# Last recurrent head: projection steps ahead of the masked copies, a later transposition of values, and a slab for the second half of the keys

## The chip, the cores and the metric

The kernel runs on one core of one Trainium2 chip. The metric is the device time of one execution in microseconds. Three runs of the kernel before took 1207.51, 1208.60 and 1209.41 us; the median is 1208.6 us. The profile is of one further execution.

## The reference, cut to what matters

One decoder layer over 1024 tokens and 1024 channels, in float32. The normed input goes through one projection `w_in`. Half of its output feeds a dilated attention of 8 heads of 64 channels, the other half a gated recurrence of 4 heads of 128 channels. Both are concatenated, go through `w_out`, and a two-layer MLP follows.

```python
proj = h @ w_in[layer]
q_a, k_a, v_a, q_h, f_h, i_h, g_h = jnp.split(proj, splits, axis=-1)
attn = dilated_mixture_attention(q_a..., k_a..., v_a..., slopes)
rec = hgrn2_recurrence(q_h, f_h, i_h, g_h, lower_bounds[layer], hgrn_out_norm[layer])
mixed = jnp.concatenate([attn, rec], axis=-1) @ w_out[layer]
```

The recurrence is, per head, `S_t = diag(f_t) S_{t-1} + (1-f_t) i_t^T` and `o_t = S_t^T q_t`, computed in chunks.

## The kernel before, in words

Every float32 matrix product is made in three passes: each operand is split into a high part (a rounding copy on ACT, `L86`) and a low part (a subtraction on DVE, `L87`), and `three_pass` issues high x low, high x high and low x high (`L90` to `L92`). So one contraction step of 128 is three matmuls of 512 columns. Below, one such step with its three matmuls is called a unit. The code counts it as 650.

The core works through the recurrent heads 0 to 3 (`hgrn_core`), then through the 64 steps of the attention's 8 heads, then through `w_out` and the MLP. All instructions stand in the order in which the code is written; each engine takes its own in that order, and a semaphore holds an instruction until what it needs is there. To keep PE busy in the recurrent heads, projections that later work needs are put between the pieces of a head. They are Python generators in `queue`; `fill(ns)` draws units from them until their costs reach `ns` (a debt is carried on), so the number in `fill` sets how many units are written at that place. In the last head (`h == 3`) the queue holds `attn_proj(0)` and `attn_proj(1)`, the projections of the first two pairs of attention heads: queries in two halves (`pm_aq`), the first half of the values (`pm_av`), both halves of the keys (`pm_ak`), the second half of the values. What a unit draws with it also goes to the other engines: at a half's end DVE reads the sum out of PSUM (`qf` at `L786`, `vf` at `L803`, `kf` at `L720`), ACT and POOL make its high and low part (`both_parts`: `hiq` or `hik`, then the subtraction in place), and SP's queue sends them on. At the fifth unit of a half of the queries, or of the values, the next weights are split, `wh` on ACT and `wl` on DVE.

`hgrn_core` itself: a prologue fills, makes sums `pd` on PE and their diagonal blocks in `at` on DVE. Then come three steps. Each step has 32 short matmuls into two banks `pl` (`L535`), a chain of updates on DVE (`qt` at `L548` and `L551`, totals at `L555` to `L557`, the next step's `qs` at `L490` and `L492`, `kt` at `L560` to `L562`), six masked copies of `pl` into `at` on DVE (`L567`), a fill of 3500 and another of 3500. The next step's `pl` needs the chain's `qs` and `kt`, not the copies; `at` is first needed after the third step. After that come `pl` 6 (`L578`), the turning of `kt` (`pk`), the states (`pu`) and the output (`po`).

`values_turn` transposes a half of the values on PE (`pvt`, `L753`), ACT and DVE copy the result into `v`, and SP stores it. For the first half of a pair's values it is drawn with the fourth unit of the first half of the keys (`n == 3` in `attn_proj`).

Buffers: PSUM has two banks per tag, and a projection's sum and `pvt` share tag `mm`. `half` is a slab of 512 columns with two buffers, for `qf`, `hiq`, `vf`, `kf` and `hik` alike. `kf` and `hik` of the first pair are free again only when the DMAs that read them have landed. Tag `P` has three buffers of 1024 columns.

After the recurrent heads the attention's 64 steps draw units by a table (`UNITS`), and at step 47 what is left of the queue is drained.

Of the kernel before, what the change touches and what calls it, by code (L numbers as in the profile page):

```python
# [9 lines left out]
F32R = mybir.dt.float32r  # L10
# [7 lines left out]
P = 128  # L18
# [8 lines left out]
HH = 4  # L27
# [10 lines left out]
def hymba_layer(ctx, tc, x, w_in, w_out, w_ff1, w_ff2, g_pre, lb_logits, g_mix, g_post,  # L38
# [464 lines left out]
    def hgrn_core(h, scale, after=None):  # L503
        hd = heads[h]
        inat, gate, prod, qt, kt, tot = (hd[n] for n in ("inat", "gate", "prod", "qt", "kt", "tot"))
        ready = quarter_sets(hd, h, 0, tot)
        fill((5900 if 0 < h < HH - 1 else 5200) * scale)
        at = slab("S", f"at{h}", F32, (P, NT, P))
        for hf in range(2):
            pd = bank("pv", f"pd{h}_{hf}")  # L510
# [14 lines left out]
        for step in range(3):  # L525
            c = 4 ** step
            nb = 32 // c
            sets, cv = ready
            got = []
            for u in range(2):  # L530
                pl = bank(("s", "t", "pv")[step], f"pl{h}_{step}{u}").rearrange("p (n q) -> p n q", n=4)
                for n in range(4):
                    qs = sets[u][:, n].rearrange("p (s w) -> p s w", s=3)
                    for g, (a, b) in enumerate(halves):
                        TE.matmul(pl[a:b, n, :96], kt[:, (4 * u + n) * P + a:(4 * u + n) * P + b],  # L535
                                  qs[:, :, 32 * g:32 * g + 32], start=True, stop=True, skip_group_check=True)
                got.append(pl)
            w = T // (4 * c)
            at_ = (0, 768, 960)[step]
            tots = totals[:, at_:at_ + 3 * w].rearrange("p (i w) -> p i w", i=3)  # L540
            u23, u123, nx = (tots[:, i] for i in range(3))
            cw = cv.rearrange("p n b f -> p (n b) f")
            q4 = qt.rearrange("p (m f c) -> p m f c", f=4, c=c)
            k4 = kt.rearrange("p (m f c) -> p m f c", f=4, c=c)

            def spread(ap, k=c):
                return ap.unsqueeze(2).to_broadcast([P, w, k])
            V.tensor_tensor(out=q4[:, :, 1], in0=q4[:, :, 1], in1=spread(cw[:, :, 0]), op=ALU.mult)  # L548
            for hf in range(2):
                n4 = slice(hf * 4, hf * 4 + 4)  # L550
                V.tensor_tensor(out=qt[:, hf * 512:hf * 512 + 512].rearrange("p (n b f c) -> p n b (f c)", n=4, f=4, c=c)  # L551
                                [:, :, :, 2 * c:],
                                in0=sets[hf][:, :, 128:].rearrange("p n (b w) -> p n b w", b=nb),
                                in1=cv[:, n4, :, 0:1].to_broadcast([P, 4, nb, 2 * c]), op=ALU.mult)
            V.tensor_tensor(out=u23, in0=cw[:, :, 2], in1=cw[:, :, 3], op=ALU.mult)  # L555
            V.tensor_tensor(out=u123, in0=cw[:, :, 1], in1=u23, op=ALU.mult)
            V.tensor_tensor(out=nx, in0=cw[:, :, 0], in1=u123, op=ALU.mult)  # L557
            if step < 2:
                ready = quarter_sets(hd, h, step + 1, nx)
            V.tensor_tensor(out=k4[:, :, 2], in0=k4[:, :, 2], in1=spread(cw[:, :, 3]), op=ALU.mult)  # L560
            V.tensor_tensor(out=k4[:, :, 1], in0=k4[:, :, 1], in1=spread(u23), op=ALU.mult)
            V.tensor_tensor(out=k4[:, :, 0], in0=k4[:, :, 0], in1=spread(u123), op=ALU.mult)  # L562
            for u, pl in enumerate(got):
                for part_, mask, c2 in ((0, own[:, 2 * step], c), (2, own[:, 2 * step + 1], 2 * c),
                                        (1, near[:, step], 2 * c)):
                    av = at[:, 4 * u:4 * u + 4, :64].rearrange("p n (b two c) -> p n b two c", two=2, c=c2)
                    V.copy_predicated(  # L567
                        av[:, :, :, 1, :],
                        mask.rearrange("p (b c) -> p b c", c=c2).unsqueeze(1).to_broadcast([P, 4, 32 // c2, c2]),
                        pl[:, :, part_ * 32:part_ * 32 + 32].rearrange("p n (b c) -> p n b c", c=c2))  # L570
            cur = nx
            table_part()
            fill(3500 * scale)
            table_part()
            fill(3500 * scale)
        pl = bank("s", f"pl{h}_6")
# [131 lines left out]
    turn_later = []  # L708
    second_done = [False] * (AH // 2)

    def both_parts(full, name):
        hi = half(f"hi{name}", F32R)
        S.activation(hi, f32(full), AF.Copy)
        G.tensor_tensor(out=full, in0=f32(full), in1=f32(hi), op=ALU.subtract)
        return hi, full

    def keys_read(pr, pm, hf):
        sl = slice(hf * 512, hf * 512 + 512)
        full = half(f"kf{pr}{hf}", F32R)
        V.tensor_tensor(out=f32(full).rearrange("p (r m) -> p r m", r=DIL), in0=classes(pm),  # L720
                        in1=rrow[:, sl].rearrange("p (r m) -> p r m", r=DIL), op=ALU.mult)
        keys_done[pr] += 1
        if pr > 0:
            key_jobs.extend((pr, i, hf, full) for i in range(2))
            return
        for q, src in zip(("kh", "kl"), both_parts(full, f"k{pr}{hf}")):
            for i, (a, b) in enumerate(halves):
                dst = f32(pairs[pr][0][i][q]).rearrange("p (r m) -> p r m", r=DIL)[:, :, hf * P:(hf + 1) * P]
                for c, d in halves:
# [35 lines left out]
    def attn_proj(pr):  # L765
# [50 lines left out]
        pairs[pr] = (stacks, vs)  # L816
        for hf in range(2):
            for n, cost in enumerate(proj_t(wk, f"ak{pr}", hf, box)):
                if n == 3 and hf == 0:
                    values_turn()  # L820
                    cost += 450.0
                yield cost
# [1469 lines left out]
```

## Time and profile before

| | |
|---|---|
| median of 3 runs | 1208.6 us |
| profiled execution, its own time | 1209.69 us |
| span from first to last instruction | 1207.9 us |
| mean granted TensorE clock | 0.997 |
| PE / DVE / ACT / POOL busy | 98% / 69% / 45% / 25% of the span |
| recurrent head 3 from `pd` to its last fill | about 240 to 303 us |
| the attention's steps | from about 304 us |

The profile counts time from the first instruction. In the windows of the trace, "PE busy" is the time in which a matmul is in flight, "PEclk" the granted clock as a share of full speed. In the timeline a row is start, duration, engine, line, operation, output from inputs, shapes, count, and in brackets how long the engine had been idle just before and whose end it had waited for. A matmul of 512 columns lasts 0.39 us there but overlaps its neighbours, so the distance between starts is the cost.

### The profile page before, as it was taken

The page shows a single profiled execution, that of the slowest core. Times are in us where ns is not written, and L with a number is a line of the kernel's source. Part 1 is how long each engine was busy: PE and PEld are TensorE (multiplying, and loading weights), DVE is VectorE, ACT ScalarE, POOL GpSimd, SP SyncE. Part 2 cuts the span into 40 slices and gives each one's busy share as a digit, 9 for nine tenths or more (in the row PEclk, how much of TensorE's full clock was granted, in tenths as well). Part 3 has the DMA queues.
Part 4 walks back from the last instruction along what each step waited for, and adds up shares of the span by engine and source line. Part 5 has one row for each costly group of instructions (what it writes and reads, how often), then busy time and mean ns, then how long its engine had stood idle before and what let it go on. Part 6 is the DMA issues. An engine that isn't in the chain of part 4 may idle for free.

```text
span 1207.9 us, 17596 instructions
## 1 busy us (share of the span) xinstructions
PE 1186.9 (98%) x6486; PEld 1008.7 (84%) x6486; DVE 838.9 (69%) x1426; ACT 548.4 (45%) x1082; POOL 296.9 (25%) x284
## 2 busy tenths in 40 slices
PE   9999999979999999999999999999999999999997
PEld 8898989857888888888888888888888888888886
DVE  5686969574666767676689566766678553578796
ACT  7633433332565668755664222232234543434562
POOL 0121212001120110143320786575631000000022
PEclk9999999999999999999999999999999999999999
DMA  5222333125645455272514555553586534533337
GB/s 217 71 67 84 97 96 97 53 82 125 147 107 134 123 147 160 56 242 105 192 62 157 183 210 190 194 190 144 198 323 264 196 105 139 169 93 105 105 105 279
DMA packets 90549, 175.49 MB, mean 145 GB/s; under 512 B 14944, under 2 KB 42464, under 8 KB 90464
## 3 DMA queue, kind: packets, MB, share of 16 engines
q1 hardware_dynamic: 90320, 174.37, 44.9%
q8 instruction: 51, 0.84, 0.3%
q14 instruction: 34, 0.28, 0.1%
q10 hardware_dynamic: 144, 0.00, 0.0%
HBM read 116.91 MB, written 47.99 MB: 137 GB/s over the span
## 4 chain that ended last, share of the span: by engine, by line
PE 89%; DVE 5%; ACT 3%; issue 1%; DMA 1%; SPq 0%; POOL 0%; DVEq 0%; POOLq 0%; ACTq 0%
PE f L2032 18%; PE f2s L2032 7%; PE pig L90 2%; PE pig L92 2%; PE pig L91 2%; PE pwo L90 2%; PE pwo L92 2%; PE pwo L91 2%; PE pl L535 1%; PE pm_aq L92 1%; PE pm_ak L90 1%; PE pm_q L90 1%; PE pm_aq L90 1%; PE pm_ak L91 1%; PE pm_ak L92 1%
## 5 line engine op out<-in xcount | busy, mean ns | idle before, releaser
L87 DVE TENSOR_TENSOR al<-ar,ah 128x1024 fp32r<-128x1024 f32 x56 | 70.6, 1261 | 80.0 <-ACT ah L86 77.6
L2032 PE MATMUL f<-bh,ah 128*128 128x512 f32 x320 | 124.5, 389 | 0.0
L2032 PE MATMUL f<-bl,ah 128*128 128x512 f32 x320 | 124.5, 389 | 0.0
L2032 PE MATMUL f<-bh,al 128*128 128x512 f32 x320 | 124.5, 389 | 0.0
L86 ACT ACTIVATE ah<-ar 128x1024 fp32r<-128x1024 f32 x56 | 59.1, 1056 | 86.6 <-DMA ar<-actd 86.3
L2032 PEld LDWEIGHTS f<-bh,ah 128*128 128x128 f32 x320 | 60.1, 188 | 12.6
L2032 PEld LDWEIGHTS f<-bl,ah 128*128 128x128 f32 x320 | 60.1, 188 | 12.5
L2032 PEld LDWEIGHTS f<-bh,al 128*128 128x128 f32 x320 | 60.1, 188 | 12.3
L2106 POOL TENSOR_SCALAR lbl<-ssq 128x1 f32<-128x1 f32 x4 | 3.3, 821 | 245.0 <-ACT fd L2102 244.8
L1655 POOL TENSOR_TENSOR e<-x,e 128x512 f32<-128x512 f32 x14 | 21.6, 1541 | 131.8 <-DVE x L1606 131.8
L2032 PE MATMUL f2s<-bl,ah 128*128 128x512 f32 (+1 forms) x128 | 48.9, 382 | 0.0
L2032 PE MATMUL f2s<-bh,al 128*128 128x512 f32 (+1 forms) x128 | 48.9, 382 | 0.0
L2032 PE MATMUL f2s<-bh,ah 128*128 128x512 f32 (+1 forms) x128 | 48.9, 382 | 0.0
L698 POOL TENSOR_SCALAR tout<-traw 128x256 f32<-128x256 f32 x16 | 18.5, 1156 | 99.2 <-DMA traw<-in_bias_tab_dram 99.2
L87 DVE TENSOR_TENSOR bl<-br,bh 128x1024 fp32r<-128x1024 f32 x32 | 40.1, 1253 | 1.2 <-ACT bh L86 1.1
L2049 ACT ACTIVATE acc<-f 128x512 f32<-128x512 f32 x28 | 16.7, 598 | 49.5 <-PE f L2032 49.5
L86 ACT ACTIVATE bh<-br 128x1024 fp32r<-128x1024 f32 x32 | 33.6, 1050 | 3.9 <-PE f L2032 2.8
L744 POOL TENSOR_TENSOR kl<-kf,kh 64x512 fp32r<-64x512 f32 x12 | 16.2, 1352 | 73.1 <-ACT kh L743 60.7
L87 DVE TENSOR_TENSOR wl<-raw,wh 128x1024 fp32r<-128x1024 f32 x21 | 25.9, 1233 | 10.7 <-ACT wh L86 10.7
L90 PE MATMUL pwo<-woh,mt 128*128 128x512 f32 x80 | 32.2, 403 | 0.0
L92 PE MATMUL pwo<-woh,mt 128*128 128x512 f32 x80 | 31.3, 391 | 0.0
L91 PE MATMUL pwo<-wol,mt 128*128 128x512 f32 x80 | 31.2, 390 | 0.0
(1720 smaller groups left out, 3901.4 us busy)
## 6 DMA issues: line engine op xcount, KB each, us to landing
ar<-actd SPq DMA_DIRECT2D x56, 512.0 KB, 3.6
br<-in_w_ff_dram SPq DMA_DIRECT2D x16, 1024.0 KB, 6.0
raw<-in_w_in_dram SPq DMA_DIRECT2D x28, 512.0 KB, 4.1
w1r<-in_w_ff_dram SPq DMA_DIRECT2D x14, 1024.0 KB, 6.4
actd<-e SPq DMA_DIRECT2D x17, 768.0 KB, 4.2
actd<-e SPq DMA_DIRECT2D x11, 1024.0 KB, 4.1
xr<-in_x_dram SPq DMA_DIRECT2D x8, 512.0 KB, 8.3
raw<-in_w_out_dram SPq DMA_DIRECT2D x8, 512.0 KB, 3.8
```

Of the source, the lines that this page charges most:

```text
L86: S.activation(hi, src, AF.Copy)
L87: eng.tensor_tensor(out=lo, in0=src, in1=f32(hi), op=ALU.subtract)
L90: TE.matmul(dst, lhs[0], rhs[0], start=start, stop=False)
L91: TE.matmul(dst, lhs[0], rhs[1], start=False, stop=False)
L92: TE.matmul(dst, lhs[1], rhs[0], start=False, stop=stop)
L535: TE.matmul(pl[a:b, n, :96], kt[:, (4 * u + n) * P + a:(4 * u + n) * P + b], qs[:, :, 32 * g:32 * g + 32], start=True, stop=True, skip_gro ...
L698: G.tensor_scalar(by_class(dst[:, part_ * w:(part_ + 1) * w]), in_blocks(raw[:, FAR * DIL:]), 8.0, None, op0=ALU.mult)
L744: G.tensor_tensor(out=kl[a:b], in0=src, in1=f32(kh[a:b]), op=ALU.subtract)
L1655: eng[0].tensor_tensor(out=e1[:, 3], in0=a21, in1=e1[:, 2], op=ALU.add)
L2032: TE.matmul(pm, a[:, j, c], b[:, j, d], start=start and j == 0 and q == 0, stop=stop and j == 1 and q == 2, skip_group_check=True)
L2049: S.activation(acc_at(p, i), pm, AF.Copy)
L2106: G.tensor_scalar(base[:, t:t + 1], sums[j][:, t:t + 1], 1.0 / D, EPS, op0=ALU.mult, op1=ALU.add)
```

## The change

Five things change, and all of them act where the last recurrent head and the projection of the first attention pair stand side by side.

1. The first fill of the last head is 6600 instead of 5200 (the others keep theirs).
2. In the last head, the first fill of 3500 of each step stands ahead of the six masked copies instead of behind them. For the other heads only a call that issues table loads moves ahead of the copies; it puts nothing on DVE.
3. The transposition of the first pair's first half of values is drawn with the seventh unit of the keys (`n == 6`) instead of the fourth.
4. The second half of the first pair's keys (`kf` and `hik`) no longer uses two buffers of `half`: both lie in one new slab of tag `P`, named `kp`.
5. `both_parts` takes the place of its high part as an argument.

```diff
-        fill((5900 if 0 < h < HH - 1 else 5200) * scale)
+        fill(5200.0 if h == 0 else 5900.0 if h < HH - 1 else 6600.0)
...
             V.tensor_tensor(out=k4[:, :, 0], in0=k4[:, :, 0], in1=spread(u123), op=ALU.mult)
+            table_part()
+            if h == HH - 1:
+                fill(3500 * scale)
             for u, pl in enumerate(got):
...
             cur = nx
-            table_part()
-            fill(3500 * scale)
+            if h < HH - 1:
+                fill(3500 * scale)
             table_part()
             fill(3500 * scale)
...
-    def both_parts(full, name):
-        hi = half(f"hi{name}", F32R)
+    def both_parts(full, name, hi=None):
+        hi = half(f"hi{name}", F32R) if hi is None else hi
...
     def keys_read(pr, pm, hf):
         sl = slice(hf * 512, hf * 512 + 512)
-        full = half(f"kf{pr}{hf}", F32R)
+        roomy = slab("P", f"kp{pr}", F32R, (P, 2, 512)) if pr == 0 and hf == 1 else None
+        full = half(f"kf{pr}{hf}", F32R) if roomy is None else roomy[:, 0]
...
-        for q, src in zip(("kh", "kl"), both_parts(full, f"k{pr}{hf}")):
+        for q, src in zip(("kh", "kl"), both_parts(full, f"k{pr}{hf}", None if roomy is None else roomy[:, 1])):
...
-                if n == 3 and hf == 0:
+                if n == (3 if pr else 6) and hf == 0:
                     values_turn()
```

What this does to the order of the instructions is shown at three places. The names are those of the text above, with a running number behind them; a number behind `pl` is the step and the bank.

DVE in the last recurrent head, from the end of the first step's chain to the start of the second's. Before:

```order
L562 TENSOR_TENSOR kt_2602<-kt_2602,tot_2815 128x256
L567 COPY_PREDICATED at_2795<-own,pl_00_2816 128x4x32
L567 COPY_PREDICATED at_2795<-own,pl_00_2816 128x4x16x2
L567 COPY_PREDICATED at_2795<-near,pl_00_2816 128x4x16x2
L567 COPY_PREDICATED at_2795<-own,pl_01_2825 128x4x32
L567 COPY_PREDICATED at_2795<-own,pl_01_2825 128x4x16x2
L567 COPY_PREDICATED at_2795<-near,pl_01_2825 128x4x16x2
L786 TENSOR_TENSOR qf_2877<-pm_aq_2808,rrow 128x512
L87 TENSOR_TENSOR wl_2904<-raw_2621,wh_2903 128x1024
L548 TENSOR_TENSOR qt_2513<-qt_2513,tot_2815 128x64x4
```

And now:

```order
L562 TENSOR_TENSOR kt_2602<-kt_2602,tot_2821 128x256
L790 TENSOR_TENSOR qf_2871<-pm_aq_2795,rrow 128x512
L570 COPY_PREDICATED at_2805<-own,pl_00_2822 128x4x32
L570 COPY_PREDICATED at_2805<-own,pl_00_2822 128x4x16x2
L570 COPY_PREDICATED at_2805<-near,pl_00_2822 128x4x16x2
L570 COPY_PREDICATED at_2805<-own,pl_01_2831 128x4x32
L570 COPY_PREDICATED at_2805<-own,pl_01_2831 128x4x16x2
L570 COPY_PREDICATED at_2805<-near,pl_01_2831 128x4x16x2
L87 TENSOR_TENSOR wl_2904<-raw_2621,wh_2903 128x1024
L548 TENSOR_TENSOR qt_2513<-qt_2513,tot_2821 128x64x4
```

The reading of the second half of the queries (`qf`) moved from behind the six copies to ahead of them; the low part of the key weights (`wl`) still stands behind them.

DVE again, from the end of the second step's chain to the start of the third's. Before:

```order
L562 TENSOR_TENSOR kt_2602<-kt_2602,tot_2815 128x64x4
L567 COPY_PREDICATED at_2795<-own,pl_10_2909 128x4x8x4
L567 COPY_PREDICATED at_2795<-own,pl_10_2909 128x4x4x8
L567 COPY_PREDICATED at_2795<-near,pl_10_2909 128x4x4x8
L567 COPY_PREDICATED at_2795<-own,pl_11_2918 128x4x8x4
L567 COPY_PREDICATED at_2795<-own,pl_11_2918 128x4x4x8
L567 COPY_PREDICATED at_2795<-near,pl_11_2918 128x4x4x8
L803 TENSOR_TENSOR vf_2961<-pm_av_2887,rrow 128x512
L757 TENSOR_TENSOR v_2886<-pvt_2980,v_2886 128x8x64
L548 TENSOR_TENSOR qt_2513<-qt_2513,tot_2815 128x16x16
```

And now:

```order
L562 TENSOR_TENSOR kt_2602<-kt_2602,tot_2821 128x64x4
L807 TENSOR_TENSOR vf_2955<-pm_av_2881,rrow 128x512
L570 COPY_PREDICATED at_2805<-own,pl_10_2915 128x4x8x4
L570 COPY_PREDICATED at_2805<-own,pl_10_2915 128x4x4x8
L570 COPY_PREDICATED at_2805<-near,pl_10_2915 128x4x4x8
L570 COPY_PREDICATED at_2805<-own,pl_11_2924 128x4x8x4
L570 COPY_PREDICATED at_2805<-own,pl_11_2924 128x4x4x8
L570 COPY_PREDICATED at_2805<-near,pl_11_2924 128x4x4x8
L761 TENSOR_TENSOR v_2880<-pvt_2989,v_2880 128x8x64
L724 TENSOR_TENSOR kf_3003<-pm_ak_2961,rrow 128x512
L548 TENSOR_TENSOR qt_2513<-qt_2513,tot_2821 128x16x16
```

The reading of the values (`vf`) moved ahead of the copies, and the reading of the first half of the keys (`kf`), which stood behind the third step's copies, now stands ahead of the third step's chain.

PE around the values' transposition. Before, with four units of the keys ahead of it (two more units like the last three rows follow before the third step's `pl`):

```order
L90 MATMUL pm_ak_2967<-hTh_89,wh_2903 128x512
L91 MATMUL pm_ak_2967<-hTl_90,wh_2903 128x512
L92 MATMUL pm_ak_2967<-hTh_89,wl_2904 128x512
L753 MATMUL pvt_2980<-ident,vf_2961 128x128 x4
L90 MATMUL pm_ak_2967<-hTh_91,wh_2903 128x512
L91 MATMUL pm_ak_2967<-hTl_92,wh_2903 128x512
L92 MATMUL pm_ak_2967<-hTh_91,wl_2904 128x512
```

And now, with seven units of the keys ahead of it:

```order
L92 MATMUL pm_ak_2961<-hTh_91,wl_2904 128x512
L757 MATMUL pvt_2989<-ident,vf_2955 128x128 x4
L90 MATMUL pm_ak_2961<-hTh_91,wh_2903 128x512
L91 MATMUL pm_ak_2961<-hTl_92,wh_2903 128x512
L92 MATMUL pm_ak_2961<-hTh_91,wl_2904 128x512
L90 MATMUL pm_ak_3016<-hTh_93,wh_2903 128x512
L91 MATMUL pm_ak_3016<-hTl_94,wh_2903 128x512
L92 MATMUL pm_ak_3016<-hTh_93,wl_2904 128x512
L535 MATMUL pl_20_3020<-qs_20_2939,kt_2602 64x96 x8
```

The transposition stands three units later, and with it the first unit of the second half of the keys (`pm_ak_3016`) now stands ahead of the third step. At the first step's `pl`, at `pl` 6 and at the output `po`, two more units have been drawn than before at the same place; they are missing at the other end, in the attention's steps 45 and 46, where the last two units of the queue stood.

## The prediction

> **What bounds the kernel now.** The page's first part comes first: PE has work in flight for 98% of the span, so only the places where it doesn't can be won.
>
> ```profile
> PE 1186.9 (98%) x6486; PEld 1008.7 (84%) x6486; DVE 838.9 (69%) x1426; ACT 548.4 (45%) x1082; POOL 296.9 (25%) x284
> ```
>
> The windows of the trace, cut at the last recurrent head's waits, show where that is. The columns are the length of the window, then busy time (and count) of each engine, the granted clock, DMA.
>
> ```profile
> 240.00:246.00 6.00, 5.03 (x46) 3.28 (x44) 4.31 (x9) 5.03 (x9) 0.00 (x0) 1.00 0.11 32
> 246.00:257.20 11.20, 9.41 (x68) 7.68 (x67) 10.70 (x24) 2.78 (x7) 1.29 (x1) 1.00 0.46 127
> 257.20:262.10 4.90, 3.24 (x13) 2.04 (x13) 3.22 (x6) 1.58 (x2) 1.27 (x1) 1.00 0.19 44
> 262.10:272.30 10.20, 5.98 (x23) 4.60 (x21) 7.88 (x25) 1.72 (x5) 0.00 (x0) 0.83 0.32 91
> 272.30:286.20 13.90, 13.90 (x98) 11.21 (x96) 5.08 (x14) 0.63 (x1) 1.29 (x1) 1.00 0.45 107
> 286.20:295.70 9.50, 7.40 (x31) 5.28 (x30) 2.28 (x4) 3.88 (x6) 1.80 (x2) 0.82 0.65 152
> 304.00:440.00 136.00, 136.00 (x820) 118.34 (x820) 87.93 (x274) 81.04 (x227) 20.82 (x17) 1.00 0.53 128
> 440.00:520.00 80.00, 78.43 (x498) 67.82 (x497) 56.75 (x166) 60.45 (x167) 11.08 (x19) 1.00 0.44 123
> ```
>
> Between 240 and 296 us PE is idle for 0.97, 1.79, 1.66, 4.22, 0 and 2.10 us, together 10.7 us, and in two windows the clock is down as well: 0.17 of 10.2 us and 0.18 of 9.5 us are, at half clock, 3.5 and 3.4 us of slow running. From 304 to 440 us PE never idles; to 520 us it idles 1.6 us. So half of the whole span's 21 us of idle PE lies in one recurrent head. What PE waits for there is read from the timeline of PE, around each wait:
>
> ```profile
> 240.32 0.40 PE L512 MATMUL pd<-prh,ones 128*128 128x512 f32 x1
> 244.25 1.81 PE L535 MATMUL pl<-qs,kt 128*64 128x96 f32 x32
> 253.37 0.39 PE L92 MATMUL pm_av<-hTh,wl 128*128 128x512 f32 x1
> 255.54 1.54 PE L535 MATMUL pl<-qs,kt 128*64 128x96 f32 x32 [1.79 <-DVE kt L562]
> 258.96 0.39 PE L92 MATMUL pm_av<-hTh,wl 128*128 128x512 f32 x1
> 261.74 0.50 PE L92 MATMUL pm_ak<-hTh,wl 128*128 128x512 f32 x1 [0.75 <-DVE wl L87]
> 262.07 0.40 PE L90 MATMUL pm_ak<-hTh,wh 128*128 128x512 f32 x1
> 263.90 0.39 PE L92 MATMUL pm_ak<-hTh,wl 128*128 128x512 f32 x1
> 268.51 1.11 PE L753 MATMUL pvt<-ident,vf 128*128 128x128 f32 x4 [4.22 <-DVE vf L803]
> 272.55 1.54 PE L535 MATMUL pl<-qs,kt 128*64 128x96 f32 x32
> 287.94 0.40 PE L92 MATMUL pm_av<-hTh,wl 128*128 128x512 f32 x1
> 294.87 0.85 PE L753 MATMUL pvt<-ident,vf 128*128 128x128 f32 x4
> ```
>
> From 262.07 to 263.90 lie eight starts: 0.228 us for one matmul of 512 columns at full clock. Transposes and `pd` are costed likewise, 0.11 and 0.23. Measured against that, the loss at each place, idle and slow running together, is:
>
> - (a) `pd`: 240.32 to 244.25 is 3.93 us for four `pd` and six others, ten starts or 2.28. Lost 1.65.
> - (b) second `pl`: 253.37 to 255.54 is 2.17 for one start. Lost 1.94.
> - (c) first unit of the keys: 258.96 to 262.07 is 3.11 for four starts, 0.91. Lost 2.2.
> - (d) first transposition of values: 263.90 to 272.55 is 8.65 for ten starts and four transposes, 2.72. Lost 5.9.
> - (e) first unit of the second pair, and slow running behind it: 287.94 to 294.87 is 6.93 for 13 starts, 2.96. Lost 4.0.
>
> Together 15.7 us. What makes the waits is on DVE and ACT:
>
> ```profile
> 254.80 0.60 DVE L562 TENSOR_TENSOR kt<-kt,tot 128x256 f32<-128x256 f32 x1
> 255.43 0.92 DVE L567 COPY_PREDICATED at<-own,pl 128x128 f32<-128x128 uint8 x2
> 257.88 0.71 DVE L786 TENSOR_TENSOR qf<-pm_aq,rrow 128x512 f32<-128x512 f32 x1
> 258.62 0.63 ACT L713 ACTIVATE hiq<-qf 128x512 fp32r<-128x512 f32 x1 [7.36 <-DVE qf L786]
> 259.16 1.04 ACT L86 ACTIVATE wh<-raw 128x1024 fp32r<-128x1024 f32 x1
> 260.23 1.45 DVE L87 TENSOR_TENSOR wl<-raw,wh 128x1024 fp32r<-128x1024 f32 x1 [1.64 <-ACT wh L86]
> 261.61 0.41 DVE L548 TENSOR_TENSOR qt<-qt,tot 128x256 f32<-128x256 f32 x1
> 265.99 0.61 DVE L567 COPY_PREDICATED at<-own,pl 128x128 f32<-128x128 uint8 x2
> 267.76 0.69 DVE L803 TENSOR_TENSOR vf<-pm_av,rrow 128x512 f32<-128x512 f32 x1
> 270.29 0.69 DVE L757 TENSOR_TENSOR v<-pvt,v 128x512 fp32r<-128x512 f32 x1 [1.83 <-ACT v L756]
> 284.60 0.69 DVE L720 TENSOR_TENSOR kf<-pm_ak,rrow 128x512 f32<-128x512 f32 x1 [7.03 <-DMA kh<-hik]
> 286.83 0.63 ACT L713 ACTIVATE hik<-kf 128x512 fp32r<-128x512 f32 x1 [8.54 <-DMA kl<-kf]
> 288.75 1.06 ACT L86 ACTIVATE wh<-raw 128x1024 fp32r<-128x1024 f32 x1
> ```
>
> In (c), `wh` stands behind `hiq` on ACT, `hiq` waits for `qf`, and `qf` stands behind six copies. In (d), `vf` stands behind the next six. In (e), the keys' second half waits 7.03 and 8.54 us for buffers of `half`, and `wh` of the second pair stands behind it on ACT.
>
> **The change part by part.**
>
> *Two units earlier (a).* Nine matmuls come ahead of `pd` and three fewer behind it. Nine starts are 2.05 us, so `pd` is reached at 242.4, when its operands are there; the next `pl` is reached at 243.95 and still waits until 244.25 for `qs`, whose chain doesn't change. Left: 0.3. Gain 1.35: six matmuls done by 244.25 that were done later before.
>
> *The second `pl` (b)* waits for `kt`, which ends at 255.40 after a chain on DVE that nothing moves. It starts at 255.54 as before, and the 1.94 stays. Gain 0.
>
> *Queries ahead of the copies (c).* `qf` starts at 255.43, 2.45 us earlier, `wh` at 256.7, and is done at 257.75. PE has one unit of values behind `pl` instead of three and wants `wh` at about 257.8: no wait. But `wl` is still behind the copies: 255.43 + 0.62 for `qf` + 2.45 for six copies gives 258.5, and the next instruction came 1.38 after `wl`'s start, so 259.9. PE's third matmul of the keys starts then at 259.95 instead of 261.74, 1.8 earlier. 1.35 of this is (a), so (c) gives 0.4 and keeps 1.8.
>
> *Values ahead of the copies, transposition three units later (d).* The second step's chain takes 265.99 - 261.61 = 4.38 us, so from 259.9 it ends at 264.3, and `vf` at 265.0. PE has 18 more matmuls ahead of the transposition: 259.95 + 0.33 + 18 x 0.228 = 264.4. It waits 0.6 instead of 4.22. Four transposes and a unit bring it to 266.25. Then the second half of the keys needs the bank that `pvt` held, which `v` on DVE frees, and that stands behind the copies: 264.9 + 1.77 (265.99 to 267.76) + 0.69 is 267.35, a new wait of 1.1. Behind this wait stand, on PE, a unit of keys and the third `pl`, which is reached at 268.2 with 27 matmuls of keys done instead of 21, that is 4.35 us earlier plus six starts. Less (a) and (c): gain 4.0, 1.9 kept. Without so long a pause there is no half clock either. Behind `v` on DVE is now `kf`, then the third step's chain; `kt` there waits for `pl` anyway.
>
> *A slab of their own (e).* `kf`'s second half needs no landing any more. It is read when PE has done the half, 21 matmuls after `pl`, at about 274.8, and `hik` is done at about 276 instead of 287.5. What is late next for `wh` on ACT is the copy out of `pl` 6: twelve matmuls and `pl` 6 itself end at about 278.3, the copy at 278.9, `wh` at 280 and `wl` at 281.2, while PE wants them at 281.2 and 281.6. That is a margin of about 0.3. The transposition's `vf` comes right behind `wl`. Left 0.2, gain 3.8. SP's eight DMAs for these keys and POOL's subtraction keep their places in their queues and come earlier. The slab's buffer is taken over by the first attention head's `pf` some 15 us after the DMAs have been issued, so nothing waits there.
>
> *Two units missing in steps 45 and 46 (f).* Here PE did waiting work:
>
> ```profile
> 452.63 0.63 ACT L743 ACTIVATE kh<-kf 64x512 fp32r<-64x512 f32 x1 [1.52 <-DVE kf L720]
> 458.78 0.45 PE L90 MATMUL pm_av<-hTh,wh 128*128 128x512 f32 x1
> 460.36 0.48 PE L90 MATMUL pm_av<-hTh,wh 128*128 128x512 f32 x1
> ```
>
> Each of the two is 0.75 us (three starts and a refill). If exponentials on ACT are the limit there, PE idles instead, at most 1.5 lost; if PE is the limit, nothing. But ACT's own wait of 1.52 for `kf` ahead of that stretch goes, since `kf` is read two units earlier. I take 0.3, near the lower end for that reason.
>
> The sum against the profiled execution: 1209.7 - 1.35 - 0.4 - 4.0 - 3.8 + 0.3 = 1200.4 us. That execution was 1.1 us above the median of the three runs (1208.6), from which the same sum gives 1199.4. The likely cause of that 1.1 is the amount of slow running, which is in (d) and (e) and goes; so neither base is quite right, and I take 1199.9.
>
> [...] The row for 286.20:295.70 has a clock of 0.82, although no wait in it exceeded 1.52 us and PE was busy for 7.4 of 9.5. The window 246.00:257.20 had a wait of 1.79 at full clock. So here a pause well under the 3.4 us of slow running can cost the clock, or not.
> [...]
> [...]
> [...]
>
> **The rivals.**
>
> 1. *The clock falls behind (b) or (c).* For: 1.9 and 1.8 us of waiting within 7 us, as much as in (e). Against: the same waits were there before at a clock of 1.00. Half of 3.4 us of slow running is 1.7: 1201.6.
> 2. *The slab waits, or `wh` is late for another reason,* so (e) stays: 1199.9 + 3.8 = 1203.7. For: the margin of 0.3, and a third user of tag `P`. Against: the order puts nothing else ahead of `wh`.
> 3. *The remaining waits are shorter,* since `wl` and `v` come earlier than I count: up to 1.8 and 1.7 more: 1196.4.
> 4. *The waits only move.* DVE is busy 10.7 of 11.2 us around the first step; if the third step is reached no earlier than before, (d) comes back as waits for `v` and `kf`. Then (a) and half of (e) remain, 3.2, and the tail takes 1.5: 1208.6 - 1.7 = 1206.9, within 0.2% of before.
> 5. *Slower.* At 452 to 465 us the queue is empty. If the last head is bound by DVE's chain throughout, so that nothing of the 15.7 goes, the missing units cost 1.5 and a pause there costs the clock once, 1.7: 1208.6 + 3.2 = 1211.8. It decides for slower if the third `pl` starts after 272.5. Against it are 3.6 us less of waiting in front of `vf` and the landings that fall away.
>
> **How the numbers follow.** Forecast (gain of 7 to 11): 0.60. Rivals 1 to 5: 0.12, 0.08, 0.10, 0.06, 0.04. The range goes from rival 3 to rival 2 with a little beyond it, 1196.5 to 1204.0; left out are half of rival 3 and rivals 4 and 5. A measurement of this kernel can tell about 0.2% (2.4 us) from no change. Faster by more: 0.60 + 0.12 + 0.08 + 0.10 = 0.90, of which I move 0.02 to no change for terms that I have not seen. Same 0.08, slower 0.04.
>
> **What would show it.** Right, if PE's waits for `vf` shrink from 4.22 to under 1, those for the second pair's `wh` and `wl` vanish, the granted clock from 262 to 296 us is 1.00, the wait of 1.8 for `kt` at the second `pl` is still there, and one of about 1 us for `v` is new. Wrong in a step, if `wl` of the keys holds PE for under 1 us or over 3, or if PE idles over 1.5 us more between 452 and 470 us. Wrong altogether, if the third `pl` starts no earlier than before.

## The result, and the profile after

| | median (range, runs) | profiled execution, its own time | span |
|---|---|---|---|
| before | 1208.35 us (1207.51 to 1209.41, 4) | 1209.69 us | 1207.9 us |
| after | 1201.39 us (1200.68 to 1202.47, 4) | 1200.68 us | 1198.6 us |

The ratio is 0.9943, with an interval of 0.9926 to 0.996: faster by 0.4 to 0.7%. The four times lie in two pairs, 1200.7 and 1202.1 to 1202.5; the profile is of one of the shorter kind.

Three views of the trace after answer to those shown of before. First the page's first part, and the windows, cut round the same waits (the last of the head runs on here to the attention's start):

```profile
PE 1182.4 (99%) x6486; PEld 1007.1 (84%) x6486; DVE 838.8 (70%) x1426; ACT 548.4 (46%) x1082; POOL 295.9 (25%) x284
```

```profile
239.40:245.40 6.00, 5.86 (x43) 4.54 (x43) 4.33 (x10) 4.69 (x10) 0.00 (x0) 1.00 0.21 58
245.40:256.90 11.50, 9.74 (x81) 7.92 (x76) 11.06 (x22) 4.12 (x9) 1.39 (x2) 1.00 0.45 124
256.90:261.50 4.60, 3.33 (x17) 2.24 (x14) 4.40 (x11) 1.90 (x5) 1.20 (x1) 1.00 0.56 121
261.50:268.70 7.20, 5.87 (x41) 4.17 (x41) 6.85 (x20) 1.24 (x3) 0.33 (x1) 1.00 0.29 94
268.70:282.00 13.30, 13.30 (x87) 10.84 (x82) 8.02 (x18) 2.92 (x4) 2.82 (x3) 1.00 0.76 176
282.00:296.00 14.00, 14.00 (x93) 12.53 (x91) 5.49 (x11) 3.99 (x7) 1.29 (x1) 1.00 0.61 160
296.00:434.00 138.00, 137.04 (x827) 119.52 (x826) 88.82 (x279) 81.42 (x230) 20.29 (x17) 1.00 0.50 125
434.00:514.00 80.00, 77.40 (x492) 67.11 (x491) 55.94 (x165) 60.63 (x167) 11.87 (x24) 1.00 0.47 135
```

PE's idle time between 240 and 296 us fell from 10.7 us to 0.14 + 1.76 + 1.27 + 1.33 = 4.5 us, and the clock there is 1.00 throughout. But the two long windows of the attention now have 0.96 and 2.60 us of idle PE, where they had 0 and 1.57. Three of PE's longest waits (what waits, releaser, total, count, longest) are the attention's, at 454.0, 304.7 and 451.3 us, and only something at 450 us was forecast:

```profile
PE ps_D L885 <- DVE stat L890: 1.2, 1, 1.2
PE ps_F L885 <- DVE stat L890: 1.0, 1, 1.0
PE pt_N L962 <- ACT pn L943: 0.8, 1, 0.8
```

Four others are the head's and were forecast. The timeline of PE gives their places:

```profile
255.48 1.54 PE L535 MATMUL pl<-qs,kt 128*64 128x96 f32 x32 [1.76 <-DVE kt L562]
259.73 0.50 PE L92 MATMUL pm_ak<-hTh,wl 128*128 128x512 f32 x1 [1.27 <-DVE wl L87]
264.72 0.66 PE L757 MATMUL pvt<-ident,vf 128*128 128x128 f32 x4 [0.37 <-DVE vf L807]
267.03 0.50 PE L90 MATMUL pm_ak<-hTh,wh 128*128 128x512 f32 x1 [0.97 <-DVE v L761]
267.92 1.54 PE L535 MATMUL pl<-qs,kt 128*64 128x96 f32 x32
```

No wait at `pd` is left, and the third `pl` starts at 267.92 where it started at 272.55. What holds PE, on DVE, and what gets the second pair's weights ready, on ACT:

```profile
258.44 1.24 DVE L87 TENSOR_TENSOR wl<-raw,wh 128x1024 fp32r<-128x1024 f32 x1
263.98 0.68 DVE L807 TENSOR_TENSOR vf<-pm_av,rrow 128x512 f32<-128x512 f32 x1
266.30 0.68 DVE L761 TENSOR_TENSOR v<-pvt,v 128x512 fp32r<-128x512 f32 x1
266.90 0.68 DVE L724 TENSOR_TENSOR kf<-pm_ak,rrow 128x512 f32<-128x512 f32 x1
```

```profile
275.24 0.63 ACT L716 ACTIVATE kp<-kp 128x512 fp32r<-128x512 f32 x1 [6.94 <-DVE kp L724]
278.92 1.06 ACT L86 ACTIVATE wh<-raw 128x1024 fp32r<-128x1024 f32 x1
```

The new wait of 1.0 for `ps_F` is at 304.7 us, in the first steps of the attention:

```profile
304.71 0.36 PE L885 MATMUL ps_F<-kh,qc 128*128 128x192 f32 x1 [0.96 <-DVE stat L890]
```

```profile
301.33 0.68 DVE L790 TENSOR_TENSOR qf<-pm_aq,rrow 128x512 f32<-128x512 f32 x1
301.92 0.68 DVE L890 CUSTOM_DVE_ANT_0 pd<-ps_D,bt 128x512 f32<-128x512 f32 x1
303.62 0.42 DVE L983 TENSOR_TENSOR ptl<-pt_D,pth 128x256 fp32r<-128x256 f32 x1 [1.01 <-ACT pth L982]
```

The second half of the second pair's queries, two units earlier, ends among the attention's first scores. So its `qf` stands ahead of `pd`, the reading of a block of 512 scores from `ps_D`, where before it stood behind it (312.44 against 310.37 us), and DVE then waits 1.01 us for ACT.

To add up losses over whole stretches, the distance from each matmul's start to the next is taken, less its undisturbed 0.227 us for 512 columns, the median in both traces (fewer columns in the same manner); waits, longer distances at the start of a unit (0.28 and 0.32 us at 458.78 and 460.36 us in before) and slow clock all count. The stretches are the last head (from 232 us), the 136 to 138 us behind it, and 80 us more:

| kernel, profiled execution | last head | attention to about 434 | to about 514 | sum |
|---|---|---|---|---|
| before | 17.5 | 1.6 | 4.3 | 23.4 |
| after | 7.2 | 2.6 | 4.8 | 14.6 |

So the head gave 10.3 us, and 1.5 went back in the attention: 8.8 of the 9.3 us by which the spans differ. (The level of each number depends on the distance taken for matmuls of few columns, the differences hardly do.)

### The profile page after: what moved, and what is told of

Same layout as the page of the kernel before. It is cut to its first block, busy times and chain, and to the rows that moved or that the text cites. A ratio compares the mean times of both kernels' runs of the same rounds, so it can differ in the third digit from the quotient of the medians.

```text
span 1198.6 us, 17591 instructions
## 1 busy us (share of the span) xinstructions
PE 1182.4 (99%) x6486; PEld 1007.1 (84%) x6486; DVE 838.8 (70%) x1426; ACT 548.4 (46%) x1082; POOL 295.9 (25%) x284
## 4 chain that ended last, share of the span: by engine, by line
PE 90%; DVE 5%; ACT 3%; issue 1%; POOL 0%; DMA 0%; DVEq 0%; POOLq 0%; ACTq 0%
PE f L2036 18%; PE f2s L2036 7%; PE pig L90 2%; PE pig L92 2%; PE pig L91 2%; PE pwo L92 2%; PE pwo L90 2%; PE pwo L91 2%; PE pm_ak L90 1%; PE pl L535 1%; PE pm_ak L92 1%; PE pm_ak L91 1%; PE pm_q L90 1%; PE pm_av L90 1%; PE pm_av L92 1%
```

## The experiments

Twelve kernels ran, in three batches; before measured 1207.93, 1207.99 and 1208.36 us in them. Intervals are of ratios to before. The question of the first four was which of the parts makes the gain.

**The slab alone,** in the kernel before.

```diff
+        roomy = slab("P", f"kp{pr}", F32R, (P, 2, 512)) if pr == 0 and hf == 1 else None
+        full = half(f"kf{pr}{hf}", F32R) if roomy is None else roomy[:, 0]
```

> The kernel before with only the slab for the second half of the first pair's keys. Theory (each part removes its own wait): PE's waits of 1.5 and 0.5 us for the second pair's weights behind the last values matmul vanish, and with them the slow running from 291.6 us; the other waits stay (1.8 for kt, 0.9 and 0.8 for the keys' weights, 4.2 for vf). About 3.8 us faster than before, 1204.5. Rival (the waits only move along DVE's chain): the wait for weights shrinks but turns up at the next place, under 1.5 us faster.

Measured: 1204.9 us, 0.9977 (0.9967 to 0.9987), 3.0 less than before. The waits for the second pair's weights are gone from its trace, the others are as they were:

```profile
259.99 0.50 PE L90 MATMUL pm_ak<-hTh,wh 128*128 128x512 f32 x1 [0.91 <-ACT wh L86]
261.47 0.50 PE L92 MATMUL pm_ak<-hTh,wl 128*128 128x512 f32 x1 [0.75 <-DVE wl L87]
268.24 1.12 PE L754 MATMUL pvt<-ident,vf 128*128 128x128 f32 x4 [4.19 <-DVE vf L804]
```

**The change without the slab.**

```diff
-        roomy = slab("P", f"kp{pr}", F32R, (P, 2, 512)) if pr == 0 and hf == 1 else None
+        roomy = None
```

> The changed kernel without the slab: the second half of the keys is in half's buffers again. Theory A (the slab carries term e): the wait for the second pair's weights is back, 3.8 us slower than the changed kernel, about 1205. Theory B (term e goes by the earlier reading of the keys' first half as well): the first half is read at about 267 instead of 277 us, so its DMAs land (6.3 and 8.5 us after the high part in the trace of before) at about 274.5 and 277, just when the second half is done; then the wait is under 0.5 us and the time that of the changed kernel, 1201 to 1202.

Measured: 1201.07 us, 0.9949 (0.9936 to 0.9962): the same as after. Beside the other parts the slab did nothing. On ACT, `hik` of the second half still waits for a landing, but it ends at 276.8 and `wh` starts at 279.00, within 0.1 of the 278.92 with the slab:

```profile
276.14 0.63 ACT L716 ACTIVATE hik<-kf 128x512 fp32r<-128x512 f32 x1 [7.76 <-DMA kl<-kf]
279.00 1.06 ACT L86 ACTIVATE wh<-raw 128x1024 fp32r<-128x1024 f32 x1
```

**The change with the turning at the fourth unit.**

```diff
-                if n == (3 if pr else 6) and hf == 0:
+                if n == 3 and hf == 0:
```

> The changed kernel with the first values' transposition at the fourth unit of the keys, as before. Theory: PE comes to it 2.05 us earlier and waits about 2.6 for vf instead of 0.4, but v stands ahead of the copies then and its wait of 1.0 vanishes: 0.9 slower than the changed kernel, or 2.6 where the longer pause costs the clock a window; 1202.3 to 1204. Rival (the place of the transposition carries term d): the whole 4 us come back, 1205.5.

Measured: 1202.69 us, 0.9962 (0.995 to 0.9974). `pvt` waits 2.4 instead of 0.4, and the wait of 1.0 for `v` is gone; by the measure of the table above the head loses 0.8 more. The profiled execution, at 1204.34 one of the two longest of five, also ran at a clock of 0.50 for 6.8 us from 454 us on, for which see the end. What makes up the rest of the 1.3 in the median is not shown.

**The change with the copies ahead of the first fill again.**

```diff
-            if h == HH - 1:
-                fill(3500 * scale)
             for u, pl in enumerate(got):
...
-            if h < HH - 1:
-                fill(3500 * scale)
+            fill(3500 * scale)
```

> The changed kernel with the six masked copies of each step ahead of the fill again, everything else as changed. Theory: qf and so wh and wl of the keys come 2.4 us later, PE's wait there grows from 1.3 to about 3.4; vf stands behind the copies and PE waits about 2.4 for it instead of 0.4; v's wait falls to about 0.5. 3.3 us slower than the changed kernel, 5 where the clock falls once: 1204.7 to 1206.5. Rival (the later transposition and the two units carry the gain): under 1 us slower.

Measured: 1204.52 us, 0.9979 (0.9971 to 0.9987), 3.1 more than after. PE waits 2.3 for `wh` of the keys, 0.5 for `wl`, 1.2 for `vf`, 0.7 for `v`. These are of an execution of 1208.14 us, which also ran slowly at 262 and at 271 us: 0.43 us from one matmul of 512 columns to the next, where it is 0.23 at 264 us. Its mean clock is 0.993, against 0.999 after. So the 3.1 holds waits and lost clock together.

The next four asked what the two units at `pd` are worth, since 0.96 and 1.03 us of new idle time lie where they are missing.

**The change with the first fill at 5200.**

```diff
-        fill(5200.0 if h == 0 else 5900.0 if h < HH - 1 else 6600.0)
+        fill(5900.0 if 0 < h < HH - 1 else 5200.0)
```

> The changed kernel with the last head's first fill at 5200 again, so without the two units ahead. Rival, as in the prediction (term a is 1.35 us of its own): the wait at pd is back, 1.35 slower less 0.3 at the tail, about 1202.4. Theory now: PE came those two units earlier to the keys' weights, whose low part DVE delivers at a fixed time, and waited 1.3 there; without them that wait falls to about 0.2 and the third matmul of the keys starts at the same time. The third pl then stands ahead of the second half of the keys, so the wait of 1.0 for v goes; and the waits of 1.0 at 304 us and of 0.8 and 1.2 at 450 us, which before did not have, go. 2 to 3 us faster than the changed kernel, 1198 to 1199, in all executions alike.

Measured: **1197.61 us** (1197.42 to 1197.68), 0.9913 (0.99 to 0.9926), 3.8 less than after: the fastest kernel of all. The timeline of PE in the head:

```profile
241.63 0.50 PE L512 MATMUL pd<-prh,ones 128*128 128x512 f32 x1 [0.66 <-ACT prh L461]
242.36 0.51 PE L512 MATMUL pd<-prl,ones 128*128 128x512 f32 x1 [0.22 <-DVE prl L463]
255.53 1.54 PE L535 MATMUL pl<-qs,kt 128*64 128x96 f32 x32 [1.76 <-DVE kt L562]
264.79 0.66 PE L757 MATMUL pvt<-ident,vf 128*128 128x128 f32 x4 [0.39 <-DVE vf L807]
265.38 1.54 PE L535 MATMUL pl<-qs,kt 128*64 128x96 f32 x32
```

The waits of 0.66 and 0.22 at `pd` are back. Nothing after them is later for it: the second `pl` starts at 255.53 (255.48 after), `pvt` at 264.79 (264.72). These times are DVE's. What is gone is 1.27 for `wl` and 0.97 for `v`, and the third `pl` starts 2.5 us earlier, 1.4 of which is that two units are still to do. The waits at 304 and 450 us are gone too.

By the measure of the table above, this execution loses 1.3 us less in the head than the profiled one of after, and 0.9 and 0.8 less in the two stretches of the attention. That is the 3.0 us by which the spans differ (1195.6 against 1198.6). The medians differ by 3.8, because that of after lies between its two pairs of times.

**The attention's table: units taken from steps 0 and 1,** so that one unit fewer is drawn in each, and the later steps have theirs.

```diff
-    UNITS = ((2, 3, 3, 4, 3, 3, 3, 3), ...
+    UNITS = ((1, 2, 3, 4, 3, 3, 3, 3), ...
```

> The changed kernel with one unit fewer in each of the attention's steps 0 and 1, so that from step 2 on the units stand as in the kernel before and the last two are in steps 45 and 46 again. Theory (the missing units cost 0.5 us of waiting at 450 us and, in about half of the executions, a half clock window there): those waits fall from 2.1 to 0.9 us, no execution shows a half clock, about 1200 in all of them; the wait of 1.0 at 304 us may move. Rival (the two times of the changed kernel come from the last head's waits): the spread of 1.7 us stays.

Measured: 1200.35 us (1199.95 to 1200.66), 0.9936 (0.9923 to 0.9949), 1.0 less than after.

**The same, taken from steps 11 and 19.**

```diff
-... (2, 3, 3, 4, 3, 3, 3, 3), (3, 3, 3, 4, 2, 3, 3, 2), ...
+... (2, 3, 3, 3, 3, 3, 3, 3), (3, 3, 3, 3, 2, 3, 3, 2), ...
```

> As the run before, but the two units are taken from steps 11 and 19, where PE never idled. Theory: the same gain at 450 us, 1200 in all executions, while the wait of 1.0 at 304 us stays. Rival: the spread of 1.7 us stays.

Measured: 1199.88 us (1199.66 to 1200.22), 0.9932 (0.992 to 0.9944), 1.5 less than after. In both the waits at 450 us are gone and the runs are 0.6 to 0.7 apart instead of 1.8; the head's losses are unchanged (7.2 and 7.1). The wait for `ps_F` at the attention's start stays here (0.9). With the units taken from steps 0 and 1 it falls to 0.5, and one of 0.4 for `ps_N` joins it.

**The change with the first two steps' copies held back behind the second step's fills, and the key weights split earlier.**

```diff
+            held.append((step, got))
...
+            if h < HH - 1 or step == 2:
+                copies()
...
+            if step == 1:
+                copies()
...
+            if pr == 0 and hf == 1:
+                w_get(A0 + 2, 0)
```

> The changed kernel with the copies of the first two steps held back behind the second step's fills, and the keys' weights split ahead of the high part of the queries, so that on DVE qf, wl, the second chain, vf and v come without a copy among them. Theory (PE's waits of 1.3 for wl, 0.4 for vf and 1.0 for v come from the copies ahead of them): all three fall, to about 0.6 in sum; about 2 us faster than the changed kernel, 1199 to 1200, and the spread of its executions stays, since that comes from 450 us. Rival (DVE's chain as a whole is the bound, so that waits only move): under 0.7 us faster.

Measured: 1201.01 us (1199.37 to 1204.8), 0.9945 (0.9932 to 0.9958), not told apart from after. The wait for `wl` goes, and 1.3 for `vf` takes its place (0.4 after); the head loses 6.2 instead of 7.2. Three of the six executions, the profiled one among them, took 1199.4 to 1199.6, 1.1 less than after's shorter pair; three took 1202.4 to 1204.8. `vf` is no longer held by the chain on DVE, which ends at 262.7, but by a buffer of `half`, which is free only when a DMA from `qf` has landed:

```profile
263.27 0.69 DVE L821 TENSOR_TENSOR vf<-pm_av,rrow 128x512 f32<-128x512 f32 x1 [0.54 <-DMA q<-qf]
```

The last four put the parts side by side.

**The first fill of 6600 alone,** in the kernel before.

```diff
-        fill((5900 if 0 < h < HH - 1 else 5200) * scale)
+        fill(5200.0 if h == 0 else 5900.0 if h < HH - 1 else 6600.0)
```

> The kernel before with the first fill of 6600 alone. The prediction's terms (a) and (f) alone: 1.35 less, 0.3 more, so 1206.9 us against 1208.0, with the waits of 4.2 for `vf` and 0.75 for `wl` about as they were. Theory D, that PE is held by DVE's times at the second `pl`, at `wl` and at `vf`, so that two units done earlier only come earlier to the next of these waits: PE's idle time at `pd` (0.97) goes, the wait for `wh` and `wl` of the keys grows from 1.65 by about 1.4, `pvt` starts at 268.5 as before, and the two units missing later add waits of 0.5 to 1.5 at 304 and 450 us: 1208.5 to 1209.5. Under 1207.2 is for the prediction, over 1208.0 for D.

Measured: 1208.32 us, 0.9998 (0.9989 to 1.0007): no change that can be told from none. By the median alone the forecast of 1206.9 isn't excluded: 1.1 less than the 1208.0 it started from is a ratio of 0.9991, just inside the interval. PE's timeline decides:

```profile
259.98 0.62 PE L90 MATMUL pm_ak<-hTh,wh 128*128 128x512 f32 x1 [2.27 <-ACT wh L86]
261.47 0.79 PE L92 MATMUL pm_ak<-hTh,wl 128*128 128x512 f32 x1 [0.43 <-DVE wl L87]
268.24 1.11 PE L753 MATMUL pvt<-ident,vf 128*128 128x128 f32 x4 [3.20 <-DVE vf L803]
```

Each of the three starts where it did with the slab alone (259.99, 261.47, 268.24), although PE came two units sooner. What the expectation missed: the second pair's weights are no longer waited for here, without any slab. So the zero is a sum. That wait went, and what came is a longer time at half clock (3.4 us from 260.2, at a clock of 0.50, and 6.8 us from 267.0, at 0.52 over 266.70 to 273.50, against 3.4 us at 0.50 twice in before) and waits of 0.9, 1.2 and 0.8 us in the attention, for `ps_F`, `ps_D` and `pt_N`. Against the slab alone, where that wait is gone as well, the two units cost 3.4 us (1208.32 against 1204.9).

**Fill 5200 and no slab,** the other parts as changed (the two edits shown above together).

> The changed kernel with the first fill at 5200 and the keys' second half in `half`, as before. Prediction's (e): the slab is what makes `hik`, and so the second pair's `wh`, early: then 2 to 4 us are lost again, 1200 to 1201. Theory B, from the kernel without the slab: as soon as the first half of the keys is read earlier, its landings are over in time, so the slab does nothing: 1197.6 within 0.4. Here the second half of the keys is read at 273.3 instead of after 275, so there is 2 us less for the landings of the first half than with 6600; a wait of 0.5 to 1.5 for the second pair's `wh` would say that the slab does matter at this fill.

Measured: 1200.3 us, 0.9939 (0.9927 to 0.9952), 2.7 more than with the slab. ACT and PE:

```profile
278.72 0.63 ACT L716 ACTIVATE hik<-kf 128x512 fp32r<-128x512 f32 x1 [7.86 <-DMA kl<-kf]
280.64 1.06 ACT L86 ACTIVATE wh<-raw 128x1024 fp32r<-128x1024 f32 x1
```

```profile
281.75 0.50 PE L90 MATMUL pm_aq<-hTh,wh 128*128 128x512 f32 x1 [0.81 <-ACT wh L86]
283.01 0.50 PE L92 MATMUL pm_aq<-hTh,wl 128*128 128x512 f32 x1 [0.53 <-DVE wl L87]
```

With the reordering and the later turning in place, the four medians are:

| | fill 5200 | fill 6600 |
|---|---|---|
| no slab | 1200.30 | 1201.07 |
| slab | **1197.61** | 1201.39 (after) |

Either part alone removes the wait for the second pair's weights; the slab does it for nothing, the two units at a price.

**Fill 5200, the diagonal products (1.71 us on DVE) moved from ahead of the first chain to ahead of its copies.**

```diff
-                V.tensor_tensor(out=at[a:b, hf * 4:hf * 4 + 4, :64], ...
+            if h < HH - 1:
+                diagonals()
...
             if h == HH - 1:
                 fill(3500 * scale)
+                diagonals()
             for u, pl in enumerate(got):
```

> The changed kernel with the first fill at 5200, and the four products that put the diagonal blocks into `at` (1.71 us on DVE) moved from ahead of the first step's chain to ahead of its masked copies. The second `pl` then waits for `kt` about 0.1 instead of 1.8, and starts at 253.8. If each wait is worth what it shows, that is 1.7 less: 1195.9. Theory D: `wl` on DVE ends at the same time as without this edit, since the products still stand ahead of it, so PE, 1.7 earlier, waits about 1.6 there; `pvt` starts at 264.8 as without it, and the time stays 1197.6 within 0.4.

Measured: 1198.23 us, 0.9918 (0.9905 to 0.9932). The second `pl` starts 1.1 earlier, and PE waits 1.58 us at `wl`, where without this edit it waits less than 0.2:

```profile
254.39 1.54 PE L543 MATMUL pl<-qs,kt 128*64 128x96 f32 x32 [0.83 <-DVE kt L570]
260.23 0.50 PE L92 MATMUL pm_ak<-hTh,wl 128*128 128x512 f32 x1 [1.58 <-DVE wl L87]
265.21 0.66 PE L766 MATMUL pvt<-ident,vf 128*128 128x128 f32 x4 [0.34 <-DVE vf L816]
```

Of the wait at the second `pl` 0.9 us was removed and nothing gained; `pvt` is no earlier (265.21 against 264.79). The second `pl` came at 254.39 and not at 253.8 as expected: one instruction of the chain, a `tot`, took 1.72 us there (248.09) instead of 0.60 (250.35 without this edit). Why is not shown.

**Fill 5200, products and copies both held back.** The edit is that of the copies held back, with `diagonals()` as the first line of `copies()`.

> The changed kernel with the first fill at 5200, the diagonal products and the masked copies of the first two steps held back on DVE until behind the second step's fills, and the key weights split ahead of them. Theory D: with 1.7 us taken from DVE's work ahead of `kt` and 4.2 more ahead of `vf`, the second `pl` starts at 253.8, `wl` ends at 257.2 ahead of PE, `pvt` starts at about 263.5 instead of 264.8, and the third `pl` at 264.1 instead of 265.4: 1.3 less, 1196.3, if the 6 us that DVE then does ahead of the third chain hide behind the fills. They end at about 273.3, when PE wants `pl` 6: a new wait of up to 1.5 there would make it 1197.5. The rival, that the time is set by PE's own work and the clock alone: 1197.6.

Measured: 1199.87 us, 0.993 (0.9916 to 0.9943). The wait for `wl` is gone and `pvt` starts at 263.82, 1.0 earlier. As in the copies held back, `vf` ahead of it waits for a buffer of `half` (1.44 us), and no longer for DVE's chain. But then:

```profile
263.07 0.69 DVE L830 TENSOR_TENSOR vf<-pm_av,rrow 128x512 f32<-128x512 f32 x1 [1.44 <-DMA q<-qf]
266.74 2.83 PE L559 MATMUL pl<-qs,kt 128*64 128x96 f32 x32 [2.26 <-DVE at L515]
```

The third `pl` uses the two banks that hold `pd`, and these are free only when the products have read them, 2.26 us after PE is ready. The profiled execution, at 1201.81 the longest of five, also ran slowly from this `pl` on, with 0.43 us from one matmul of 512 columns to the next until 272.2 instead of 0.23; the `pl` itself lasts 2.83 us instead of 1.54. Its mean clock is 0.996, against 1.000 at fill 5200 alone. The expectation had overlooked the banks and the buffer, so this run doesn't say what DVE's earlier chain is worth. A version with the products in time and only the copies held, at fill 5200, wasn't tried.

## Why the prediction was right, and where it was wrong

The total was right: the terms give 1209.7 - 9.3 = 1200.4 us for the profiled execution, which took 1200.68. The median, 1201.39, is 1.5 above the 1199.9 forecast and within the range. But two errors of opposite sign hide in it, so that the total came out so close is in part luck: (a) and (f) together were to give 1.05 us and cost 3.8, and (c) and (d) gave 7.3 where 4.4 was forecast. The two profiled executions help as well, since that of before lies 1.3 above its median and that of after 0.7 below. The signs that it named came out as said, and none of them tests whether (a) pays.

**(a) is the step that failed.** "Six matmuls done by 244.25 that were done later before" is what the trace shows, and it was priced at 1.35 us gained. With the other parts in place, undoing (a) made the kernel faster by 3.8 (3.0 between the profiled executions, of which 1.3 lie in the head), and (a) alone in the kernel before made no difference that could be told, although there it also removed the wait of (e). The reason is that PE, from there to `pvt`, waits three times for a time that DVE sets. Work done ahead of such a wait makes the wait longer. `pvt` shows it best: it is drawn from the queue itself, so the same matmuls have been done when it starts, and it starts at the same time with the two units and without, at 268.24 and 268.24 in the kernel before (with the slab in the second), at 264.72 and 264.79 with the other parts. That is the mechanism of rival 4, for this term alone. The prediction saw this for `pl` and for `wl` ("1.35 of this is (a)") but still counted the 1.35 once, as if those units had been saved and not only moved.

**(b)** stayed, as said: 1.76 idle at 255.48 (255.54 forecast).

**(c) and (d)** came out in the kernel after as worked out: 1.27 left for `wl` (1.8 forecast, `pm_ak` at 259.73 against 259.95), 0.37 for `vf` (0.6), 0.97 for `v` (1.1), the third `pl` at 267.92 (268.2). But the two waits "kept" here, `wl` and `v`, belong to (a): with fill 5200 both are gone. Credited with that, (c) and (d) are worth 1204.9 - 1197.6 = 7.3 us beside the slab, not 4.4; by the medians the copies' place is 3.1 of after's gain and the later turning 1.3, both with some lost clock in them.

**(e)** was sized well: 3.8 forecast, 3.0 measured for the slab alone. `hik` was done at 275.9 ("about 276"), `wh` at 280.0 ("280"). Its cause was half wrong, because the slab isn't the only way. With fill 6600 the first half of the keys is read at 266.9, ahead of the third chain; with 5200 it is read behind it (269.5), and its landings come that much later. So in the kernel after the slab is idle insurance, and at fill 5200 it is worth 2.7.

**(f)** was too small. The idle time at 450 us came where it was forecast; it grew by 1.03 us, and the loss in the table by 0.5, against 0.3. That at 304 us, 0.96 us more, wasn't forecast: the prediction followed the two missing units to the queue's end, but not the second pair's `qf`, which moved two units earlier into the start of the attention. Giving the units back from the attention's table brought 1.0 to 1.5 by the medians, and took away the waits at 450 us.

**Rival 1,** a lost clock behind (b) or (c), didn't happen in the profile of after, whose clock is 1.00 in every window from 239 to 514 us. It did happen in the first fill of 6600 alone, behind (c), where the wait was 2.27 + 0.43 and the clock 0.50 from 260.21 to 263.62. That the pair of longer executions of after, 1.6 us apart from the others, lost the clock at 454 us is likely: 3.4 us at half clock, as before had it twice, is 1.7, the same waits lost it in the run with the turning at the fourth unit (below), and the spread went when the waits at 450 us went. But no longer execution of after was profiled, and the mean clocks on record, 0.998 and 0.999 for the longer pair and 0.999 for both of the shorter, are too coarse to decide. So this is argued and not shown.

**Half clock** was not expected at (d) "without so long a pause", and after had none there (1.00 from 261.50 to 296 us). But it doesn't take so long a pause: the row 286.20:295.70 of before has 0.82 with no wait above 1.52 us, and the runs below have 0.50 behind a longest wait of 2.27 and of 1.2.

## What to carry to other kernels

When an engine waits several times in a row for times that another engine sets, work done sooner ahead of them is not a gain: trace it to the last of these waits, and price what its absence costs where it was taken from, at the start of the next stage as well as at the end of the queue. Test each part of a combined change by taking it out, not only by adding it alone: two parts here did the same job, one was free and the other cost 3 to 4 us. A sum that comes out right is no proof of its terms.

## What the runs showed of the hardware

In these traces the clock also fell to half behind stretches in which PE was busy for part of the time, and the same waits cost it in one kernel and not in the next. In before it was 0.50 from 268.06 to 271.47 us, behind 3.41 us without a matmul in flight, and from 291.95 to 295.36 us, behind 3.41 us in which PE was busy for 1.56. In each window below the length comes first, then PE's busy time; the clock is third from the end. The first fill of 6600 alone, at the waits for `wh` and `wl` of the keys:

```profile
256.80:260.21 3.41, 1.14 (x5) 0.66 (x5) 1.70 (x5) 1.58 (x2) 1.15 (x1) 1.00 0.02 5
260.21:263.62 3.41, 2.98 (x7) 1.86 (x7) 3.22 (x8) 1.12 (x4) 0.12 (x1) 0.50 0.81 166
```

Of the change with the turning at the fourth unit, at the waits of 1.2 for `ps_D` and 0.7 for `pt_N`:

```profile
450.82:454.23 3.41, 1.83 (x15) 1.36 (x14) 2.86 (x6) 3.35 (x11) 0.00 (x0) 1.00 0.00 0
454.23:461.06 6.83, 6.43 (x23) 5.85 (x24) 5.34 (x17) 3.26 (x9) 0.00 (x0) 0.50 0.56 147
```

Of after, with waits of 1.2 and 0.8 there, cut alike:

```profile
450.82:454.23 3.41, 1.74 (x13) 1.50 (x14) 3.24 (x9) 3.39 (x10) 0.00 (x0) 1.00 0.01 1
454.23:461.06 6.83, 6.83 (x47) 6.18 (x47) 6.46 (x21) 5.32 (x13) 0.00 (x0) 1.00 0.56 155
```

And of the copies held back, at the wait of 1.8 for the second `pl`:

```profile
252.14:255.55 3.41, 1.59 (x9) 1.01 (x8) 3.13 (x9) 0.05 (x1) 0.00 (x0) 1.00 0.37 115
255.55:258.97 3.42, 3.42 (x41) 2.96 (x42) 3.42 (x5) 0.63 (x1) 1.54 (x1) 1.00 0.23 54
```

In the first fill alone PE was busy for 1.14 of the 3.41 us ahead, and the clock was 0.50 in the next 3.41. With the turning at the fourth unit it was busy for 1.83, and the clock was 0.50 in the next 6.83. In after it was busy for 1.74 of the same stretch, and with the copies held back for 1.59 of 3.41; both stayed at 1.00. So PE's busy time in the stretch ahead does not by itself tell these four cases apart: half clock came behind 1.14 and 1.83 us, and not behind 1.59 and 1.74. What else counts is open.
